# The first FFN of a hybrid block: context products beside latent products on shared weight pages, for half of the tile pairs

## The chip, the cores and the metric

The kernel runs on one core of one Trainium2 chip. Its engines work side by side: TensorE (PE; the loading of its weights is a row of its own, PEld), VectorE (DVE), ScalarE (ACT), GpSimd (POOL) and SyncE (SP), whose queue issues nearly all DMA transfers here. The metric is the device time of one execution in microseconds; of several runs the median counts. Beside the runs there is one profiled execution, from which all rows of the profile come.

## The reference

One layer over 1024 latent tokens and 256 context tokens, D_MODEL = 1024, D_FF = 2816, float32. Cut to what matters here:

```python
def ffn_sublayer(h, shift, scale, gate, g, w_in, w_out):
    hn = modulate(rmsnorm(h, g), shift, scale)
    a, b = jnp.split(hn @ w_in, 2, axis=-1)
    y = (jax.nn.silu(a) * b) @ w_out
    return h + 0.5 * gate[:, None, :] * y

h  = ffn_sublayer(h,  mods[0], mods[1], mods[2], g_ffn1, w_ffn1_in, w_ffn1_out)      # latents
hc = ffn_sublayer(hc, mods_c[0], mods_c[1], mods_c[2], g_ffn1, w_ffn1_in, w_ffn1_out)  # context, same weights
# then projections of both streams, a bidirectional mLSTM, a spatial-gating branch, a merge,
h  = ffn_sublayer(h, mods[6], mods[7], mods[8], g_ffn2, w_ffn2_in, w_ffn2_out)
return rmsnorm(h, g_final)
```

Latents and context pass through the same weights of the first FFN; only the latents pass through the second one.

## The kernel before

**Numbers as pairs.** Every float32 operand of a matmul is split into a high part (a cast to fp32r by ScalarE) and the remainder (a subtraction by VectorE), `split`, L139 to L141. A product is three matmuls: high x high, high x low, low x high. A "page" is a tile of 128 partitions with both parts, `[128, 2, 512]` for the latents' factors and `[128, 2, w]` for weights.

**Latent products in seven steps.** The latent products of both FFNs are computed by a Strassen-like scheme: 1024 x 1024 tokens and channels are taken as 2 x 2 blocks of 512, and seven block products with sums and differences of blocks take the place of eight. `Factors` (L244) makes the factor pages: products 1 and 2 need only the first half of the tokens (`early`), products 5, 6, 7, 4, 3 need differences with the second half (`late`). `Gate` (L287) makes the input products of an FFN. Its 22 output tiles f are taken in pairs (kp, kp + 11); for a tile the steps run in the order `SEQ = (1, 6, 5, 7, 2, 4, 3)`. The first three tiles, the "head", run step by step side by side (`HSEQ`), because their later factors are still being made. A step is one page of weights, split into a ring slot, times four factor pages: 12 matmuls of 128 x 512, all on L351. `Gate.load` issues the load of a tile's two raw pages at its step 1 and forms the sums and differences of weight blocks on POOL in place (L316 to L336); `depth` steps are loaded and split ahead. `Gate.step` (L363 to L387) adds the banks together on VectorE; `Gate.out` (L390) makes the seven factors of the FFN's hidden activation of each pair and stores them, partly already split, to DRAM.

`Out` and `Stage.outp` do the same for the output products: seven products in the order `OSEQ = (1, 2, 4, 7, 6, 5, 3)`, each over 11 pages kp and four rows m, three matmuls each, on L469.

**The context in the first FFN** does not share anything with this. The class `Weights` streams all 44 weight pages of w1i once more, two raw pages and three split pages in flight, and the loop `for f in range(NF)` (L846 to L878) multiplies each with the eight context pages `hnc`: 44 pages x 8 x 3 = 1056 matmuls of 128 x 256 on L166. ScalarE and VectorE form silu(a) * b (L874, L875), split it and store it to `gcsp`. Beside this loop run the statistics, the scaling and the early factor pages of the latents (L804, L192, L193, L238, L239, and the splits). Only then does `A.gate` begin, with the latents in place. After the latents' output products a second loop over the 22 tiles (L970) reads `gcsp` back, loads and splits w1o once more (`wload`, `wsplit`) and makes all eight rows of the context's output: 528 matmuls of 128 x 256. The context's norm follows.

**What sets the order.** Work that need not be done at once is put in the list `todo`. `pump(w)` is called after each group of three matmuls and takes items from it by a credit: an item's cost (512 by default; `slow` and `later` give other values) says how many columns of matmuls lie between two items. `tick` calls do the same for the adaptive-norm weights (`ada_steps`): one load of 256 KB and one or two accumulations on VectorE. The framework's planner then orders the instructions of each engine: the place in the code is the priority, and an instruction that is ready may go ahead of one that is not. Memory is handed out from pools with a fixed number of buffers by tag, and a tile waits until the buffer before it is free.

**Names that the prediction uses.** `raw` (weights as loaded), `hl`, `ring`, `wring` (split weights), `fa`, `fb`, `fc` (factor pages of products 1 and 2, of 5 and 6, and of 7, 4, 3), `qa`, `qb` (banks of `Gate`), `po` (banks of `Out`), `pa`, `pb` (banks of the context's input products), `pc` (of its output rows), `fhl`, `fsp` (stored factors), `adapg` (adaptive-norm weights), `fo` (rows of the result). The last rows are made by `post3`, `fin2` and `put` (L1869 to L1886): a row update and a square for each of four row groups, a norm, and eight rows out, part of them by ScalarE and POOL.

## Time and profile before

| | us |
|---|---|
| median of 3 runs | 2768.88 (2764.06 to 2770.13) |
| the profiled execution, whole | 2752.25 |
| its span (the profile's time axis) | 2750.5 |
| mean granted TensorE clock in it | 0.993 |

A row of a group names the line, the engine, the operation, the tile it writes and those it reads, the count, the busy time with the mean in ns, and the idle time of the engine just before, with what ended it. A row of the timeline begins with start and length in us; one of the waits reads "who <- for whom: us in total, times, longest". In a row of the stretches stand the borders, the length, each engine's busy time with its count of instructions, the granted TensorE clock, the DMA engines' busy share and what they moved in GB/s.

### The profile page before, as it was taken

What the parts mean: (1) busy time and instruction counts of PE and PEld (TensorE: products, weight loads), DVE (VectorE), ACT (ScalarE), POOL (GpSimd) and SP (SyncE); (2) the same over time, 40 slices, a digit from 0 to 9 for tenths busy, and PEclk for the clock granted to TensorE, in tenths of its full rate; (3) what the DMA queues carried; (4) which work ended last, traced back from release to release, by engine and by line L of the source; (5) the groups of instructions that cost most, each with busy time, mean ns of one, the idle gap of its engine ahead of it and who ended that gap; (6) DMA issues with size and microseconds to landing.
All of it is one profiled execution on the core that took longest, in us unless ns stands there. A gap on an engine that the chain in (4) does not pass through costs nothing.

```text
span 2750.5 us, 35573 instructions
## 1 busy us (share of the span) xinstructions
PE 2663.2 (97%) x12652; PEld 2205.5 (80%) x12652; DVE 1946.7 (71%) x3291; ACT 1075.0 (39%) x1826; POOL 589.8 (21%) x551
## 2 busy tenths in 40 slices
PE   8899999999999999999999999999999999999997
PEld 4887788888888878877777888888877788888886
DVE  4887888787968646667665677778478866676755
ACT  3564333334336525453333333112145333333432
POOL 0102232320000121233332315443011323330001
PEclk9999999999999999999999999999999999999999
DMA  8862444439668321236554357547341333337644
GB/s 283 280 202 74 145 146 143 141 132 330 203 212 277 121 92 57 100 129 216 169 175 146 108 176 262 192 164 259 120 138 54 127 127 111 134 119 250 202 159 167
DMA packets 198434, 456.74 MB, mean 166 GB/s; under 512 B 20465, under 2 KB 46833, under 8 KB 198257
## 3 DMA queue, kind: packets, MB, share of 16 engines
q1 hardware_dynamic: 198256, 454.47, 48.4%
q8 instruction: 100, 1.64, 0.2%
q14 instruction: 78, 0.63, 0.1%
HBM read 328.95 MB, written 125.51 MB: 165 GB/s over the span
## 4 chain that ended last, share of the span: by engine, by line
PE 43%; DVE 8%; issue 4%; DMA 3%; POOL 2%; ACT 1%; SPq 0%; POOLq 0%; ACTq 0%; DVEq 0%
PE qb L351 9%; PE pt L1607 9%; PE pq L1180 7%; PE po L469 6%; PE qa L351 4%; PE pr L1099 3%; PE pu L1472 2%; PE pn L1720 2%; DVE ring L141 2%; DMA adapg<-in_w_ada_dram 1%; PE pn L1718 1%; POOL rawq L1146 1%; PE pkc L1160 1%; POOL rawq L1145 1%; DVE adacc L698 1%
## 5 line engine op out<-in xcount | busy, mean ns | idle before, releaser
L140 ACT CAST ring<-rawq 128x512 fp32r<-128x512 f32 x432 | 265.4, 620 | 592.7 <-PE qb L351 146.6
L141 DVE TENSOR_TENSOR ring<-rawq,ring 128x512 fp32r<-128x512 f32 x432 | 332.0, 774 | 213.4 <-ACT ring L140 211.6
L469 PE MATMUL po<-gring,wring 128*128 128x512 f32 x1848 | 422.6, 391 | 2.1 <-DMA gring<-fsp 2.1
L469 PEld LDWEIGHTS po<-gring,wring 128*128 128x128 f32 x1848 | 346.6, 188 | 75.2 <-issue 3.1
L351 PE MATMUL qb<-fc,ring 128*128 128x512 f32 x1440 | 344.3, 393 | 16.6 <-DVE u L371 8.3
L351 PEld LDWEIGHTS qb<-fc,ring 128*128 128x128 f32 x1440 | 272.0, 190 | 76.8 <-DVE y L374 10.6
L351 PE MATMUL qa<-fa,ring 128*128 128x512 f32 x1056 | 253.3, 390 | 0.5 <-ACT ring L140 0.5
L351 PEld LDWEIGHTS qa<-fa,ring 128*128 128x128 f32 x1056 | 198.1, 188 | 42.4 <-ACT ring L140 0.9
L351 PE MATMUL qb<-fb,ring 128*128 128x512 f32 x984 | 229.6, 390 | 0.0
L1180 PE MATMUL pq<-fc,ring 128*128 128x512 f32 x864 | 213.8, 395 | 4.5 <-DVE py L1193 3.4
L351 PEld LDWEIGHTS qb<-fb,ring 128*128 128x128 f32 x984 | 184.9, 188 | 38.2
L1180 PEld LDWEIGHTS pq<-fc,ring 128*128 128x128 f32 x864 | 160.7, 188 | 41.0 <-issue 2.7
L140 ACT CAST wring<-rw 128x512 fp32r<-128x512 f32 x154 | 95.8, 622 | 229.1 <-PE po L469 187.6
L1607 PE MATMUL pt<-yp,ring 128*128 128x512 f32 x768 | 184.3, 397 | 0.0
L141 DVE TENSOR_TENSOR wring<-rw,wring 128x512 fp32r<-128x512 f32 x154 | 108.1, 702 | 95.5 <-ACT wring L140 95.2
L1607 PEld LDWEIGHTS pt<-yp,ring 128*128 128x128 f32 x768 | 144.2, 188 | 29.2
L1180 PE MATMUL pq<-fa,ring 128*128 128x512 f32 x576 | 143.9, 398 | 1.7 <-ACT px L1186 1.5
L1180 PE MATMUL pq<-fb,ring 128*128 128x512 f32 x576 | 138.7, 394 | 1.6 <-DVE ring L141 1.6
L1180 PEld LDWEIGHTS pq<-fa,ring 128*128 128x128 f32 x576 | 108.2, 190 | 25.7 <-ACT px L1186 3.0
L1180 PEld LDWEIGHTS pq<-fb,ring 128*128 128x128 f32 x576 | 107.0, 188 | 26.3 <-DVE ring L141 3.7
L698 DVE SCALAR_TENSOR_TENSOR adacc<-adapg,sc,adacc 128x512 f32<-128x512 f32 x140 | 113.7, 824 | 17.9 <-DMA adapg<-in_w_ada_dram 16.9
L140 ACT CAST ring<-rawt 128x512 fp32r<-128x512 f32 x64 | 39.5, 619 | 185.5 <-PE pt L1607 178.0
(334 smaller groups left out, 4416.9 us busy)
## 6 DMA issues: line engine op xcount, KB each, us to landing
adapg<-in_w_ada_dram SPq DMA_DIRECT2D x144, 256.0 KB, 3.6
fsp<-fhl SPq DMA_DIRECT2D x66, 512.0 KB, 2.8
gring<-fsp SPq DMA_DIRECT2D x66, 512.0 KB, 3.5
raw<-in_w1i_dram SPq DMA_DIRECT2D x44, 512.0 KB, 4.4
graw<-fsp SPq DMA_DIRECT2D x88, 256.0 KB, 3.5
rawq<-in_w1i_dram SPq DMA_DIRECT2D x38, 512.0 KB, 3.8
rawq<-in_w2i_dram SPq DMA_DIRECT2D x38, 512.0 KB, 3.2
fsp<-x SPq DMA_DIRECT2D x66, 256.0 KB, 2.1
```

The source lines that it names most:

```text
L140: S.copy(hl[:, 0, :], src)
L141: V.tensor_sub(hl[:, 1, :], src, hl[:, 0, :].bitcast(F32))
L351: T.matmul(pt, hl[:, x, sl], pages[p][k][:, y, :], start=first and i == 0, stop=i == 11, skip_group_check=not first)
L469: T.matmul(pt, w[:, x, sl], g[:, y, :], start=grp and kp == 0 and i == 0, stop=kp == NFP - 1 and i == 2, skip_group_check=not grp)
L698: eng.scalar_tensor_tensor(acc, pgt, sc2[:, q, k:k + 1], acc, ALU.mult, ALU.add)
L1099: T.matmul(self.pt[m], pg[:, x, sl], hl[:, y, :], start=first and k == 0 and i == 0, stop=k == 3 and i == 2, skip_group_check=not first)
L1145: G.tensor_tensor(b2, b2, b1, ALU.subtract)
L1146: G.tensor_tensor(a1, a1, b2, ALU.add)
L1180: T.matmul(pt, hl[:, x, k * 128:(k + 1) * 128], pg[k][:, y, :], start=first and k == 0 and i == 0, stop=k == 3 and i == 2, skip_group_chec ...
L1472: T.matmul(pu[:, 0:257], ksl[:, kt * 128:(kt + 1) * 128], wv, start=True, stop=True)
L1607: T.matmul(pt, hl[:, x, k * 128:(k + 1) * 128], pg[:, y, :], start=kh + k + i == 0, stop=kh == 1 and k == 3 and i == 2)
L1720: T.matmul(pn[:, 0:257], qi[:, c_, :], self.C[d][:, c_, :], start=False, stop=c_ == 1)
```

## The change

In the first FFN 11 of the 22 tiles ("alone": the two of the head and the last nine) keep their context products in a loop before the latents' products. For the other 11 the context products are made inside `Gate`: the split pages of steps 1, 2 and 4 and of a new step 8 (the block b1 as loaded) are multiplied with the context pages right behind the latent products of the step. The class `Weights` goes; the loop takes half pages from a ring of twelve (four `ring` pages and eight of the second factor pool), with four raw pages, ten half pages ahead. The head has two tiles instead of three, whose raw pages the loop has already loaded.

```diff
     class Gate:
-        def __init__(self, name, raw, ring, depth, sums, pairs, head):
+        def __init__(self, name, raw, ring, depth, sums, pairs, head, alone=None, ctx=None):
...
+            self.alone = fs if alone is None else fs[:head] + fs[2 * pairs + head - alone:]
+            self.steps = [(f, p) for p in HSEQ for f in self.head] + [
+                (f, p) for f in fs[head:] for p in (SEQ if f in self.alone else SEQ[:1] + (8,) + SEQ[1:])]
...
+        def ticks(self, f):
+            if f in self.alone:
+                return (7,) if len(self.alone) < len(self.fs) else (1, 7)
+            return (5,) if self.fs.index(f) < len(self.head) + 3 else (1, 5, 2)
...
+            elif p == 8:
+                src = self.half(f, 1)[0]
...
-            for k in range(4):
+            for k in range(4 if p != 8 else 0):
...
+            if f not in self.alone and p in (1, 2, 8, 4):
+                if p == 1:
+                    self.K[f] = mm_ps("pk")
+                ctx_mm(self.K[f], hl, 0 if p in (1, 2) else 1, 0 if p in (1, 8) else 1)
+                if p == 4:
+                    ctx_out(f, self.K.pop(f))
```

```diff
+    def ctx_mm(pt, hl, j, kh):
+        for k in range(4):
+            for i, (x, y) in enumerate(((0, 0), (0, 1), (1, 0))):
+                T.matmul(pt[:, j * 256:(j + 1) * 256], hl[:, x, k * 128:(k + 1) * 128], hnc[kh * 4 + k][:, y, :],
+                         start=j + kh + k + i == 0, stop=kh == 1 and k == 3 and i == 2, skip_group_check=True)
+            pump(256)
...
+    COVER = 11
+    A = Stage("1", "w1i", 0, True)
...
+    A.q = Gate("w1i", lambda f: rawpg(), A.ring, 4, lambda n: t2(n), NFP, 2, COVER)
...
+    for i, f in enumerate(alone):
...
+        bank = mm_ps("pk")
+        for j in range(2):
+            for kh in range(2):
+                f_, j_, kh_, hl = cready.popleft()
+                ctx_mm(bank, hl, j, kh)
+                cfill(10)
+        ctx_out(f, bank)
...
-    A.gate(A.F.late(fpage, lambda k: []), tick)
+    A.gate(A.F.late(A.fpage, lambda k: [it(n1[1].inplace, k, s0, b0)]), tick)
```

The context pages now stay in memory through the whole of `A.gate`. To make room, the stage's additional ring of three pages goes (`ring2` 3 to 0, so `q.depth` is 4 throughout instead of 7), the page of stored factors `fhl` has one buffer instead of two, and the latents' first rows share their pages with factor 3. The statistics of the latents (`stats`) are paced with cost 640 instead of 1024; the scaling of the second half of the tokens (`n1[1].inplace`) moves from the loop into the late list.

In the output products, products 1 and 2 multiply their split pages also with the stored context activations, which gives rows 0 to 3 of the context's output:

```diff
+                    if gc is not None:
+                        if p == 1 and kp == 0:
+                            cps = [sm_ps("pc") for _ in range(2)]
+                        rows_mm(cps, w, gc, p == 1 and kp == 0, p == 2 and kp == NFP - 1)
+                        if p == 2 and kp == NFP - 1:
+                            self.ctx[1](cps)
```

The loop behind them keeps only rows 4 to 7: it loads and splits the other half of each page of w1o and reads `gcsp` a second time. The context's residual goes through a DRAM buffer `hcsp`, and its norm is made later, in the v projection, whose order is now products 1, 2, 7, 4, 6, 5, then the context's v steps (which load wv a second time), then 3. `Factors.late` makes the factors for these projections in another order (5 and 7 first, then 4, 6 and 3), at cost 1280 instead of 832. In `Rows` product 7 takes the banks that 6 and 5 had, and these those of the others; the vs projection runs in the order `USEQ = (1, 7, 2, 4, 6, 5, 3)`.

The end of the second FFN is changed too. The last four pages of product 3 run in two halves of 256 columns, each with its own norm and rows; the sum of squares is made by matmuls straight from the squares instead of VectorE additions; rows 5 to 7 are scaled ahead by ScalarE and multiplied by POOL, the others by VectorE; the first half of the tokens goes through VectorE alone.

```diff
+                for hx in range(halves if p == 3 else 0):
+                    cs = slice(hx * 512 // halves, (hx + 1) * 512 // halves)
+                    for m, pt in enumerate(pts):
+                        for p_, kp_, w, g, _ in list(self.ready)[:group]:
+                            tile_(pt, kp_, m, w, g, cs)
+                        post3(m, pt, hx, cs)
...
+    class Tail(Norm):
+        def sq(self, d, last):
+            sq = t2("sq")
+            S.activation(sq[:, :self.nt], self.h[d], AF.Square)
+            for j in range(self.nt // 128):
+                T.matmul(self.p4[:, j:j + 1], sq[:, j * 128:(j + 1) * 128], ones[:, 0:1], start=False, stop=last,
+                         skip_group_check=True)
...
     B.outp("w2o", lambda: xpage("raw", "graw", (128, 512)), lambda: B.rpage("gring"), hgate[:, 1, 0, :],
-           bc, lambda n_, d: put(n_, 0, d, d % 4 < P0), fin2, lambda tb, d, t: None)
+           lambda n_: n_.bcast(), lambda n_, d: put(n_, 0, d, False), fin2, lambda tb, d, t: None, halves=2, first=scaled)
```

Within the second FFN's output products `pump` then counts 256 instead of 512 for each group of three matmuls, and the two last groups of items have half their cost.

431 lines of the change are left out of this document (254 added, 177 removed).

## The prediction

> **What bounds the kernel now.** I read the head of the page first, then busy time in stretches cut at the stage borders that the timeline of TensorE shows, then the waits of the first stage.
>
> ```profile
> span 2750.5 us, 35573 instructions
> PE 2663.2 (97%) x12652; PEld 2205.5 (80%) x12652; DVE 1946.7 (71%) x3291; ACT 1075.0 (39%) x1826; POOL 589.8 (21%) x551
> ```
>
> ```profile
> fsp<-fhl SPq DMA_DIRECT2D x66, 512.0 KB, 2.8
> ```
>
> ```profile
> core 0: us, PE busy (x) PEld busy (x) DVE busy (x) ACT busy (x) POOL busy (x), PEclk, DMA share, GB/s
> 8.90:42.30 33.40, 33.40 (x86) 8.20 (x86) 7.61 (x24) 5.96 (x9) 0.73 (x1) 1.00 1.07 363
> 42.30:199.30 157.00, 142.38 (x1094) 135.69 (x1094) 128.78 (x215) 90.65 (x147) 11.77 (x9) 0.98 0.72 235
> 199.30:256.70 57.40, 57.40 (x252) 47.25 (x253) 42.65 (x53) 23.14 (x40) 17.82 (x11) 1.00 0.17 57
> 256.70:300.00 43.30, 35.67 (x148) 28.29 (x148) 42.08 (x59) 16.46 (x30) 13.36 (x8) 0.96 0.54 184
> 300.00:634.40 334.40, 330.74 (x1455) 272.45 (x1454) 261.10 (x372) 115.38 (x196) 93.04 (x63) 1.00 0.43 148
> 634.40:849.50 215.10, 212.87 (x944) 175.57 (x943) 175.54 (x302) 94.40 (x163) 0.00 (x0) 1.00 0.71 239
> 849.50:916.10 66.60, 65.65 (x539) 64.75 (x538) 60.69 (x107) 43.80 (x78) 0.00 (x0) 1.00 0.83 291
> 916.10:1031.00 114.90, 112.30 (x498) 89.06 (x497) 59.13 (x97) 44.27 (x82) 27.95 (x23) 0.99 0.22 79
> 2733.00:2750.50 17.50, 3.12 (x10) 1.47 (x10) 6.53 (x16) 3.26 (x6) 3.72 (x3) 0.64 0.32 120
> ```
>
> The kernel is a stream of matmuls: TensorE is busy in 97% of the span, so a change pays only where it removes matmuls, or where TensorE now stands. The rows are, in order: start-up; the first FFN's context products alone; the head of its latent products (21 steps of three output tiles); the first steps behind the head; the other latent products; the output products; the context's output rows; the v projection and gates; the end. The stretch 42.30 to 199.30 is the worst of the long ones, and its waits say why.
>
> ```profile
> ACT hl L140 <- DMA raw<-in_w1i_dram: 20.3, 18, 3.1
> DVE hl L141 <- ACT hl L140: 14.8, 26, 1.3
> PEld pb L166 <- DVE hl L141: 12.4, 16, 2.1
> ```
>
> Read upwards: the weight loads of TensorE wait for VectorE's half of the split, that for ScalarE's, that for the load; and a load needs one of only two raw pages back from VectorE. It is a round trip through two buffers, with VectorE busy 128.78 of 157.
>
> **Prices.** A matmul of 512 columns in the full stretch: 330.74/1455 = 0.227 us, 2.73 for a step of 12. One of 256 columns: 24 from 65.24 to 68.12, 0.120 us.
>
> ```profile
> 65.24 3.04 PE L166 MATMUL pa<-hnc,hl 128*128 128x256 f32 x24
> 68.12 0.43 PE L166 MATMUL pb<-hnc,hl 128*128 128x256 f32 x2
> ```
>
> ```profile
> 1047.36 1.60 PE L1160 MATMUL pkc<-hnc,ring 128*128 128x256 f32 x12
> 1048.79 2.91 PE L1180 MATMUL pq<-fa,ring 128*128 128x512 f32 x12
> 1051.54 1.59 PE L1160 MATMUL pkc<-hnc,ring 128*128 128x256 f32 x12
> ```
>
> The last three rows are the later k projection, which already mixes context with latent products as the change will: 12 narrow matmuls from 1047.36 to 1048.79, 0.119 each. Mixing makes them no cheaper, so I carry 0.120 on both sides. [...]
>
> **The change, part by part.** It removes no matmul: 11 of 22 tiles keep their 48 context matmuls alone, 11 x 48 = 528 move beside latent products. What goes is 22 loads of 512 KB and their splits, against 11 new half-page splits (step 8).
>
> (1) First stage and head, to the head's last product. The statistics and page splits of the latents, covered by 157 us until now, get only 528 x 0.120 = 63 us of matmuls, so the sum must be made on VectorE.
>
> ```profile
> L141 DVE TENSOR_TENSOR hl<-raw,hl 128x1024 fp32r<-128x1024 f32 x41 | 51.6, 1262 | 14.8 <-ACT hl L140 14.8
> L238 DVE SCALAR_TENSOR_TENSOR h<-h,smod,rb 128x512 f32<-128x512 f32 x16 | 11.8, 740 | 0.0
> L804 DVE TENSOR_TENSOR h<-h,pos 128x512 f32<-128x512 f32 x16 | 11.1, 718 | 1.1 <-DMA h<-in_xT_dram 1.1
> L263 DVE TENSOR_TENSOR h<-h 128x512 f32<-128x512 f32 x16 | 10.7, 687 | 0.0
> L141 DVE TENSOR_TENSOR gc<-sil,gc 128x256 fp32r<-128x256 f32 x21 | 9.9, 474 | 3.3 <-ACT gc L140 3.3
> L193 DVE TENSOR_TENSOR acc<-acc,sq 128x512 f32<-128x512 f32 x14 | 9.6, 689 | 0.8
> L875 DVE TENSOR_TENSOR sil<-sil,pb 128x256 f32<-128x256 f32 x22 | 9.2, 416 | 3.7 <-PE pb L166 2.3 <-issue 1.3
> ```
>
> ```profile
> L768 DVE TENSOR_TENSOR mods<-adc,vec 128x4 f32<-128x4 f32 x6 | 0.7, 157 | 6.8 <-PE adc L764 6.8
> ```
>
> ```profile
> 52.58 1.88 DVE L804 TENSOR_TENSOR h<-h,pos 128x512 f32<-128x512 f32 x3
> ```
>
> VectorE from 42.3 to 256.7 did 128.78 + 42.65 = 171.4. Off go 22 page splits x 1.262 + 11 x (0.416 + 0.474) = 37.6, and the third head tile's 7 splits and 7 sums, 14 x 0.69 (L263, L193) = 9.7. Half-page splits in place of page splits add 44 x 0.69 - 22 x 1.262 = 2.6. Remains 126.7 at mean durations; back to back the engine does better (three in 1.88 us, 0.63 for 0.72 mean), at the least 126.7 x 0.63/0.69 = 115.7. I take the middle, 121, and 10 us of its own waits: the 6.8 on the conditioning stay, those for pages shrink with four raw pages and twelve half-page slots. The head then ends at 42.3 + 131 = 173.3. TensorE's own work would allow 42.3 + 63 + 14 x 2.73 = 144, so VectorE sets it. The fair comparison is 256.7 less what the new kernel does later, 63.4 and one head tile of 7 x 2.73 = 19.1: 174.2. So **-1**. Bounds: 115.7 and 8 of waits, 166 (-8); VectorE no better fed than before (171.4 of 214.4, 80%), 126.7/0.80 = 158 and 201 (+27).
>
> Start-up has two pages instead of three among the conditioning weights while the queue runs at 363 GB/s: 0.52 MB, **-1** (0 to -1.4).
>
> (2) Latent products behind the head. 133 steps x 2.73 = 363 in 377.7: 14.7 lost.
>
> ```profile
> PE qb L351 <- DVE y L374: 8.3, 4, 4.2
> PE qb L351 <- DVE u L371: 3.0, 3, 2.0
> ```
>
> ```profile
> 2164.02 4.79 PE L351 MATMUL qb<-fc,ring 128*128 128x512 f32 x12 [5.29 <-DVE u L371]
> ```
>
> All of it is VectorE behind with the sums; VectorE is busy 42.08 of 43.30 just after the head. Eleven tiles now have 48 x 0.120 = 5.8 us more TensorE work each and 0.69 + 0.89 more on VectorE, so its share falls: (303 + 16 for the extra tile + 17)/(382 + 63) = 76% for 80%. But the new head also carries the scaling of the second half of the latents (8 x 0.74, L238) in the late list, as the second FFN's head does, which stood 5.29. I leave 6 of the 14.7: **-9** (-14 to 0). Added waits: the weight ring is 4 deep instead of 7, raw pages still 4; the head ran on 4 without a gap (57.40 of 57.40), so 0. The stored factor pages go from two buffers to one. A late store (2.8 us) would hold ScalarE's next cast and behind it VectorE's split; the stores are three items of cost 1152 apart, 3 x 1152/512 x 0.68 = 4.6 us, so 0 (to +8 if each of 11 pairs lost 0.7).
>
> (3) Output products and context rows. 264 x 0.120 = 31.7 go to the first two products, 31.7 stay, with some 2 of the norm's matmuls (priced as L199 and L207 in part 4). 33.7 + 31.7 = 65.4 for 66.6. VectorE loses 22 splits, 15; its 60.7 - 15 = 46 now lie over 34 us of matmuls, so 12 us run on beside the first two v products (96 x 0.227 = 21.8, with 8 splits, 5.5): hidden with 4 us to spare. In the first two products DMA gains 22 reads of 256 KB, but they take 31.7 us longer. **-2** (-4 to +8). The context norm leaves the place where 2.6 us stood (112.30 of 114.90) and runs under the later v products; the second reading of wv, 4.2 MB, goes into a stretch at 79 GB/s: **-1** (-2.6 to +3). The new order of the vs products: its stretch shows no idle TensorE, 0.
>
> (4) The end. The last block runs in halves of 256 columns.
>
> ```profile
> 2715.26 5.95 POOL L1872 TENSOR_TENSOR fo<-fo,rbs 128x512 f32<-128x512 f32 x4 [222.16 <-ACT fo L1871]
> 2723.90 9.09 PE L469 MATMUL po<-gring,wring 128*128 128x512 f32 x39 [1.76 <-DMA gring<-fsp]
> 2735.28 1.05 PE L199 MATMUL p<-ones,acc 128*128 128x1 f32 x8 [2.29 <-DVE acc L193]
> 2738.59 2.07 PE L207 MATMUL rb<-diag,ones 128*128 128x512 f32 x2 [2.26 <-DVE diag L203]
> 2741.32 3.38 DVE L1874 SCALAR_TENSOR_TENSOR fo<-h,vec,rb 128x512 f32<-128x512 f32 x5 [2.78 <-ACT rbs L1880]
> 2742.04 3.72 POOL L1872 TENSOR_TENSOR fo<-fo,rbs 128x512 f32<-128x512 f32 x3 [20.83 <-ACT fo L1871]
> ```
>
> From 2733.0 to 2750.5: 2.3 to the sums, 3.3 to the broadcast, 2.7 to the rows, 4.4 for these (to 2745.76), 4.7 for the last store. At half width I price a VectorE or ScalarE step at 0.42, as L875's narrow product above: row update and square without an addition 1.1 with the gaps, sums and root 2.8 (two diagonal blocks of four), broadcast and copy 1.7, five rows x 0.42 = 2.1, store 4.7: 12.4, so -5.1; 96 x 0.120 - 48 x 0.227 = +0.6. The other half's rows leave POOL, where 5.95 us held the store queue and behind it the load that TensorE missed for 1.76: -1.5. **-6** (-8 to +6, the latter if the new sums of squares, matmuls between the row groups, are waited for: 7 x about 1.7).
>
> **Sum.** -1 - 1 - 9 - 2 - 1 - 6 = -20 on a span of 2750.5 (2752.25 with what lies around it). The median of the runs, 2768.88, stands 16.6 above that execution; I carry the difference to it: **2749**.
>
> **The rivals.** *VectorE starves the first stage* (slower). The latents' preparation has 94 us less cover; if VectorE is fed no better than before, the head ends at 201, +27 for -1: 2749 + 28 = 2777. For it: 80% busy then, much of it ACT before DVE. Against: the two-page round trip is gone. It decides once the head ends later than 193. [...]
>
> *All holes fill*: part 1 at 166, no loss behind the head, both ends of 3 and 4: -8 - 1 - 14 - 4 - 3 - 8 = -38, 2731. For it: VectorE falls to 71% in the shared tiles. Against: its bursts at a pair's end stay.
>
> *The loads bind*: 20 pages, x in, x out, the products' stores and the next tile's pages, 10.5 + 4.2 + 4.2 + 2.9 + 1.0 = 22.8 MB, at the stage's 235 GB/s take 97 us of the 131; VectorE waits some 10 more: 2759.
>
> *It only moves work*: no matmul goes, and what the first stage saves comes back as waits in its head; without the gains of 1 and 2 only 3 and 4 remain, -9, and the single factor page takes 6 of its 8: 2766.
>
> **How the numbers follow.** Forecast 0.52, starved 0.15, holes filled 0.15, loads 0.08, only moved 0.10. About 0.2%, 5.5 us, is what a measurement tells from no change: faster is under 2763.3, slower over 2774.4. Faster has the forecast, the filled holes and most of the loads case, 0.73; same the moved case and some, 0.11; slower the starved one, 0.16. The range, 2726 to 2776, reaches to the filled holes and up to the starved case; the forecast's own is 2736 to 2762.
>
> **What would show it.** Right: context products alone over by about 115 to 130, VectorE busy above 90% there, the head done near 173 (wrong if past 190); no wait over 3 us behind it; 0.119 to 0.120 us per narrow matmul beside wide ones; context rows down to 34 us; 13 us from the last product to the end. Wrong, as a whole, if TensorE's idle time before the head's end exceeds 45 us, or if the last block shows matmuls waiting at each row.

## The result and the profile after

The changed kernel takes **2783.4 us** in the median of 5 runs (2776.5 to 2789.3), the kernel before 2768.4 beside it (5 runs): a ratio of 1.0053, 95% interval 1.0039 to 1.0066. It is slower by 15 us; the prediction, 2749 with a range up to 2776, was wrong in sign and in range. The profiled execution of after took 2783.5 us.

The head of the profile of after, then that of a second execution of the kernel before, which took 2763.8 us (the one shown ahead of the prediction took 2752.25, 16 below the median; from here on I compare with this second one):

```profile
span 2780.6 us, 35770 instructions
...
PE 2684.3 (97%) x12734; PEld 2222.9 (80%) x12734; DVE 1909.7 (69%) x3294; ACT 1049.1 (38%) x1820; POOL 580.9 (21%) x550
```

```profile
span 2762.0 us, 35573 instructions
...
PE 2670.8 (97%) x12652; PEld 2207.5 (80%) x12652; DVE 1943.0 (70%) x3291; ACT 1074.7 (39%) x1826; POOL 592.7 (21%) x551
```

TensorE is busy 13.5 us longer. The new end adds 82 small matmuls, and the block that holds them accounts for 5.1 us of this (216.76 for 211.68 in the rows below). So a good part of the loss is not idle time: the same matmuls run slower. The granted clock says it too, 0.985 against 0.992: (1 - 0.985) x 2780.6 - (1 - 0.992) x 2762.0 = 20 us of full clock that after does not get, an upper bound, since a low clock costs nothing where TensorE stands.

Busy time by stretch, cut at the stage borders: first after, then before (second execution). The rows of after are the context alone, the head, the other latent products, the output products with half of the context rows, the other half, the v projection to the first k product, k projection to the vs projection, the output products of the second FFN, and the end.

```profile
41.60:117.70 76.10, 72.60 (x556) 71.28 (x556) 67.53 (x139) 51.59 (x106) 6.21 (x6) 0.93 0.72 247
117.70:177.40 59.70, 46.42 (x181) 33.68 (x180) 54.28 (x90) 26.70 (x48) 15.61 (x10) 0.91 0.17 58
177.40:633.40 456.00, 448.38 (x2213) 379.75 (x2212) 322.90 (x475) 153.82 (x268) 104.81 (x77) 1.00 0.43 145
633.40:887.00 253.60, 247.83 (x1208) 209.28 (x1207) 181.37 (x308) 96.67 (x163) 0.00 (x0) 0.99 0.65 213
887.00:925.30 38.30, 34.96 (x276) 33.07 (x274) 33.80 (x62) 23.48 (x42) 0.52 (x1) 1.00 0.93 317
925.30:1048.90 123.60, 115.52 (x494) 90.98 (x495) 74.31 (x114) 52.00 (x97) 33.07 (x23) 0.96 0.39 129
1048.90:1517.20 468.30, 448.07 (x2023) 364.48 (x2022) 297.66 (x460) 195.78 (x323) 129.26 (x115) 0.97 0.43 142
...
2551.20:2768.40 217.20, 216.76 (x1020) 181.45 (x1019) 143.28 (x242) 85.48 (x153) 2.12 (x3) 1.00 0.60 196
2768.40:2780.60 12.20, 2.15 (x9) 1.26 (x9) 3.83 (x13) 0.99 (x3) 2.09 (x3) 0.58 0.40 132
```

```profile
43.50:204.80 161.30, 145.20 (x1094) 137.27 (x1093) 129.02 (x215) 90.50 (x147) 12.60 (x9) 0.97 0.72 229
...
262.20:639.70 377.50, 366.64 (x1602) 300.64 (x1601) 302.08 (x430) 131.65 (x226) 106.86 (x71) 1.00 0.45 152
639.70:855.80 216.10, 213.60 (x945) 175.44 (x944) 175.33 (x302) 94.32 (x162) 0.00 (x0) 1.00 0.72 238
...
922.90:1036.10 113.20, 110.59 (x497) 87.77 (x496) 59.12 (x97) 44.29 (x82) 27.96 (x23) 1.00 0.23 81
1036.10:1499.20 463.10, 444.78 (x2022) 361.87 (x2021) 295.70 (x458) 195.91 (x323) 130.74 (x115) 0.99 0.43 143
...
2531.30:2744.50 213.20, 211.68 (x935) 174.40 (x933) 140.33 (x225) 84.89 (x146) 5.95 (x4) 1.00 0.61 198
```

After less before, by borders: start-up 41.6 for 43.5, -1.9. First context product to first output product, 591.8 for 596.2, -4.4. First output product to first v product, 291.9 for 283.2, **+8.7**. From there to the first k product, 123.6 for 113.2, **+10.4**. The k stretch, whose work is the same, 468.3 for 463.1, +5.2. Up to the second FFN's output products +1.9. These 217.2 for 213.2, +4.0. The end 12.2 for 17.5, -5.3. Together +18.6 between these two executions; between the medians it is 15. Each stretch here and below comes from one profiled execution, and the same program can differ by 6.6 us in a single stretch, as the first run shows.

### The profile page after: what moved, and what is told of

It reads as the page before. It is cut to its first block, busy times and chain, and to the rows that moved or that the text cites. A ratio compares the mean times of both kernels' runs of the same rounds, so it can differ in the third digit from the quotient of the medians.

```text
span 2780.6 us, 35770 instructions
## 1 busy us (share of the span) xinstructions
PE 2684.3 (97%) x12734; PEld 2222.9 (80%) x12734; DVE 1909.7 (69%) x3294; ACT 1049.1 (38%) x1820; POOL 580.9 (21%) x550
## 4 chain that ended last, share of the span: by engine, by line
PE 45%; DVE 7%; issue 4%; DMA 2%; POOL 2%; ACT 1%; SPq 0%; POOLq 0%; DVEq 0%; ACTq 0%
PE qb L362 9%; PE pq L1295 9%; PE pt L1757 8%; PE po L494 6%; PE qa L362 4%; PE pr L1214 3%; PE pu L1621 2%; PE pn L1870 2%; DVE ring L109 1%; DMA adapg<-in_w_ada_dram 1%; PE pn L1868 1%; PE pkc L1275 1%; POOL rawq L1261 1%; POOL rawq L1260 1%; ACT ring L108 1%
## 5 line engine op out<-in xcount | busy, mean ns | idle before, releaser
L109 DVE TENSOR_TENSOR ring<-rawq,ring 128x512 fp32r<-128x512 f32 x453 | 338.5, 752 | 238.4 <-ACT ring L108 233.7
L108 ACT CAST ring<-rawq 128x512 fp32r<-128x512 f32 x453 | 277.6, 620 | 570.1 <-PE qb L362 160.1
L494 PE MATMUL po<-gring,wring 128*128 128x512 f32 (+1 forms) x1896 | 429.2, 385 | 1.1 <-DMA gring<-fsp 0.4
L362 PE MATMUL qb<-fc,ring 128*128 128x512 f32 x1464 | 352.3, 393 | 12.9 <-DVE u L391 12.9
L1295 PE MATMUL pq<-fc,ring 128*128 128x512 f32 x864 | 220.2, 403 | 8.0 <-DVE py L1308 5.7
L346 POOL TENSOR_TENSOR rawq<-rawq 128x512 f32<-128x512 f32 x41 | 55.9, 1365 | 294.2 <-DVE ring L109 294.2
```

Of the source, the lines that this page charges most:

```text
L108: S.copy(hl[:, 0, :], src)
L109: V.tensor_sub(hl[:, 1, :], src, hl[:, 0, :].bitcast(F32))
L346: G.tensor_tensor(a2, a2, a1, ALU.subtract)
L362: T.matmul(pt, hl[:, x, sl], pages[p][k][:, y, :], start=first and i == 0, stop=i == 11, skip_group_check=not first)
L494: T.matmul(pt[:, cs], w[:, x, sl], g[:, y, cs], start=grp and kp == 0 and i == 0, stop=kp == NFP - 1 and i == 2, skip_group_check=not grp)
L1295: T.matmul(pt, hl[:, x, k * 128:(k + 1) * 128], pg[k][:, y, :], start=first and k == 0 and i == 0, stop=k == 3 and i == 2, skip_group_chec ...
```

## The experiments

Ratios are to the kernel before, run beside each. The second and third rows start from the kernel before, all later ones from the changed kernel.

| edit | median, us | ratio, 95% interval |
|---|---|---|
| the change itself | 2783.4 | 1.0053, 1.0039 to 1.0066 |
| before, once more | 2764.8 | 0.9994, 0.9980 to 1.0008 |
| before with the new end alone | 2766.2 | 0.9998, 0.9987 to 1.0009 |
| no sharing of pages | 2771.3 | 1.0013, 1.0002 to 1.0025 |
| no position values | 2769.9 | 1.0009, 0.9996 to 1.0021 |
| norm sums of the latents later | 2778.1 | 1.0032, 1.0019 to 1.0044 |
| half of the low parts on GpSimd | 2782.7 | 1.0048, 1.0035 to 1.0061 |
| all context rows in the second pass | 2778.1 | 1.0040, 1.0026 to 1.0054 |
| context pages on GpSimd's queue | 2776.4 | 1.0030, 1.0021 to 1.0040 |
| first loads in the general ring | 2778.1 | 1.0036, 1.0022 to 1.0050 |
| ... and on GpSimd's queue | 2781.6 | 1.0046, 1.0031 to 1.0061 |
| ... with the context pages too | 2783.0 | 1.0060, 1.0043 to 1.0076 |
| context norm's sums later | 2773.4 | 1.0021, 1.0009 to 1.0033 |
| four differences on VectorE | 2777.4 | 1.0038, 1.0024 to 1.0053 |
| twelve differences on VectorE | 2773.1 | 1.0012, 1.0001 to 1.0023 |
| three edits together, loads on SyncE | **2759.6** | **0.9963**, 0.9950 to 0.9976 |
| ... on GpSimd's queue | 2767.2 | 0.9989, 0.9977 to 1.0001 |
| another three, loads on GpSimd's queue | 2766.0 | 0.9995, 0.9984 to 1.0006 |
| ... on SyncE | **2759.2** | **0.9970**, 0.9958 to 0.9982 |

### The kernel before, once more

> The kernel before, unchanged, profiled once more. Theory A (the profiled execution of before was a lucky one: the half-clock stretches of TensorE, 24 us of them between 42 and 2740 us, depend on where short waits fall): another execution shows 40 us or more of half clock and a span of 2760 or more, and the stretch from the first k-projection product to the first vs product, 456.6 us in the first profile, is 4 to 10 us longer although the order of instructions is the same. Rival B (the clock is a property of the kernel): 24 us of half clock again, span 2750, 456 to 458 us.

Its rows are those shown above, and theory A held in its times, with a span of 2762.0 us; its reason, where short waits fall, these rows do not show. The k stretch took 456.5 us at clock 1.00 in the first execution and 463.1 at 0.99 in this one, with the same program:

```profile
1031.00:1487.50 456.50, 439.30 (x2022) 358.42 (x2021) 296.74 (x459) 195.85 (x323) 129.83 (x115) 1.00 0.43 145
```

So a difference of 5 us in that stretch is no cost of the change that one could point to. Over all profiles of this study it lies between 456.5 and 469.4, the longest belonging to a version that beats after as a whole; whether the change makes it long more often is not shown: the three profiles of before and of before with the new end have 456.5 to 463.2, the seventeen of after and its variants 460.3 to 469.4.

### The new end alone

The kernel before, with the halves, the sums of squares by matmuls and the new sharing of the last rows.

> The kernel before with the new end of the second FFN alone. Theory: the end from the last product shrinks from 17.5 to 12.4 as in the changed kernel and the halves cost 3 to 4 us in the products ahead, so 1 to 3 us faster than before. Rival (the added sums of squares, matmuls between the row groups, eat all of it): no difference or slower by up to 4.

End 11.6 us for 17.5, but the products ahead of it 216.9 for 213.2, and no measurable gain. In after one sees where it goes (timeline of TensorE):

```profile
2756.70 0.50 PE L230 MATMUL p<-ones,sq 128*128 128x1 f32 x4
2757.07 0.72 PE L494 MATMUL po<-gring,wring 128*128 128x256 f32 x4
...
2769.41 0.61 PE L230 MATMUL p<-ones,sq 128*128 128x1 f32 x4 [0.69 <-ACT sq L228]
```

They are not waited for, as I had feared: only 0.69 us behind the last square. But four sums of one column cost 2757.07 - 2756.70 = 0.37 us, and eight such groups stand between products, 3.0 us. With the broadcast of the first half, 0.5, and the halved matmuls, 0.6, this makes 4.1 us for the +4.0 of that block. A wait for a load there is also 1.1 us shorter than in before, so about 1 us stays unexplained.

### No sharing

```diff
-    COVER = 11
+    COVER = 22
```

All 22 tiles make their context products ahead of the latents', in the changed kernel's memory and with its ring of half pages.

> The changed kernel with all 22 tiles' context products alone again (still half pages, four raw pages, ring of twelve, head of two): none beside latent products. Theory V (VectorE is the limit until the head's end; sharing pages saves VectorE's splits but the cover is lost as well, so the input stage gains nothing): first output product at 633 +- 6 us, as in the changed kernel and before, total within 6 us of the changed kernel. Rival S (sharing pays as it saves 22 page loads and splits): the first output product comes 10 to 20 us later, total 10 to 20 us slower than the changed kernel.

```profile
42.70:189.80 147.10, 140.78 (x1093) 138.81 (x1093) 131.29 (x263) 101.02 (x199) 7.57 (x6) 0.94 0.69 228
189.80:230.20 40.40, 38.64 (x170) 31.42 (x169) 37.19 (x48) 11.71 (x21) 18.00 (x11) 1.00 0.56 179
230.20:622.30 392.10, 384.47 (x1686) 316.53 (x1685) 307.30 (x435) 137.25 (x234) 106.37 (x75) 1.00 0.45 149
```

From the first context product to the first output product it takes 579.6 us, for 591.8 in after and 596.2 in before. Neither forecast came about: the first output product is 11 us earlier, not at the same time and not later. Up to this border the rest of the change (more raw pages, half pages, the smaller head, the other pacing, none of them tried alone) gains 16.6 us, and the sharing gives 12.2 of it back. But the border moves: the output products then wait and take 293.8 us. From the first context product to the first v product it is 873.4 us without sharing, 883.7 in after, 879.4 in before (873.8 in its first execution). So the sharing costs 10 to 12 us, which the medians confirm (2771.3 for 2783.4), and of the gain of the rest at most 6 us are left there. Where the sharing loses: up to the head's end the matmuls at the prices of the prediction are 1056 x 0.120 + 14 x 2.73 = 164.9 of 187.5 without sharing (22.6 lost), and 528 x 0.120 + 38.2 = 101.6 of 135.8 with it (34.2 lost): 11.6. Behind the head 392.1 - 140 x 2.73 = 9.9 are lost without sharing and 456.0 - 382.2 - 63.4 = 10.4 with it. The wide cover of narrow matmuls behind the head bought nothing.

### VectorE in the first stage

Three runs. The first leaves out the 16 additions of the latents' position values.

```diff
-            slow(add_pos, tb, d, cost=640)
```

> The changed kernel without the addition of the position embedding (16 VectorE additions of 128x512, 16 x 0.69 = 11 us, left out). Theory V (VectorE sets the end of the head, 177.4 us): the head ends 8 to 12 us earlier and the first output product 6 to 12 us earlier, the total likewise. Rival C (the order on TensorE sets it: the norm's matmuls wait for the sums while ready products stand behind them): the head ends less than 4 us earlier.

The head ends 126.5 us after the first context product, 135.8 in after: -9.3 for 16 additions of some 0.68 us. The second run puts the norm sums of the second half of the latents nine places later in TensorE's order, because after shows a wait for them, and slow matmuls behind it, thirteen at 0.384 us for 0.227:

```profile
117.73 1.55 PE L362 MATMUL qa<-fa,ring 128*128 128x512 f32 x6
126.40 1.84 PE L167 MATMUL p<-ones,acc 128*128 128x1 f32 x8 [7.12 <-DVE acc L162]
128.10 4.99 PE L362 MATMUL qa<-fa,ring 128*128 128x512 f32 x13
```

```diff
-        todo.extend([nop, n1[tb].rstd, nop, nop, n1[tb].bcast])
+        todo.extend([nop] * (10 if tb else 1) + [n1[tb].rstd] + [nop] * 2 + [n1[tb].bcast])
```

> The norm sums of the second half of the latents are put nine places (about 6 us of matmuls) later in the first stage's order. Theory of a wait: the 7.12 us wait just behind the start of the latent products and the half clock behind it are a cost of the order, the head ends 5 to 10 us sooner (gate start to head end 59.6 -> 50 to 55), and the time falls by 5 to 10 us against 2783. Rival, the theory of VectorE: the head's end is set by VectorE's work (the run without position additions moved it by 9.3 us with 9.6 us of additions left out), so the wait only moves to another place: the head end stays within 3 us of 135.8 us after the first context product, and the time within 3 us of 2783.

```profile
132.53 1.20 PE L180 MATMUL rb<-diag,ones 128*128 128x512 f32 x2 [1.94 <-DVE diag L176]
...
139.54 6.72 PE L362 MATMUL qb<-fb,ring 128*128 128x512 f32 x20 [1.77 <-ACT fb L108]
```

The wait of 7.12 is down to 0.95, and others stand in its place; the head ends at 138.2 us after the first context product, no sooner. VectorE sets it.

Why the sums are late in after can be read from its trace. From 114.3 to 127.4 us GpSimd forms sums and differences of weight blocks, eight operations back to back, and beside them VectorE takes up to 1.78 us for what takes it 0.69 elsewhere:

```profile
120.67 3.37 POOL L344 TENSOR_TENSOR rawq<-s,rawq 128x512 f32<-128x512 f32 x2
```

```profile
121.17 1.75 DVE L162 TENSOR_TENSOR acc<-acc,sq 128x512 f32<-128x512 f32 x1
```

Seven operations of VectorE between 114.66 and 126.25 us lose 7.2 us in all, as much as TensorE waits. In before the same additions took 689 ns (L193 in the prediction), ahead of GpSimd's work. No run moved GpSimd's operations here, so this is a reading of the trace; the v projection below has the test of the same link.

The third run gives GpSimd every second low part of the context's pages:

```diff
-        split(hl, craw[f, j][:, kh * 512:(kh + 1) * 512])
+        src = craw[f, j][:, kh * 512:(kh + 1) * 512]
+        S.copy(hl[:, 0, :], src)
+        (G if cring[0] % 2 else V).tensor_tensor(hl[:, 1, :], src, hl[:, 0, :].bitcast(F32), ALU.subtract)
```

> Half of the low parts of the first stage's split pages (those of the context alone, about 22 subtractions of 0.6 us) are made by GpSimd instead of VectorE. Theory: VectorE sets the first stage; with some 13 us of work off it the head ends 6 to 13 us sooner after the first context product (135.8 -> 123 to 130) and the time falls by 5 to 12 us against 2783. Rival: GpSimd holds VectorE up while it runs, as in the v projection, and is slower itself: the head ends at 132 to 145 and nothing is gained.

The head ends at 139.6. Groups of VectorE up to there, first of this run, then of after (count, busy us, mean ns):

```profile
L894 DVE TENSOR_TENSOR hl<-rawc,hl 128x512 fp32r<-128x512 f32 x16 | 16.1, 1012 | 1.8 <-ACT hl L893 1.8
L916 DVE TENSOR_TENSOR h<-h,pos 128x512 f32<-128x512 f32 x14 | 13.8, 995 | 0.2 <-DMA h<-in_xT_dram 0.2
```

```profile
L109 DVE TENSOR_TENSOR hl<-rawc,hl 128x512 fp32r<-128x512 f32 x32 | 21.3, 705 | 1.7 <-ACT hl L108 1.7
...
L914 DVE TENSOR_TENSOR h<-h,pos 128x512 f32<-128x512 f32 x14 | 9.5, 684 | 0.0
```

Half of the instructions left VectorE, but of 21.3 us only 5.2, because the rest run at 1012 ns instead of 705; the position additions, which nobody touched, lose 4.3. From 42 to 118 us GpSimd is busy for 31.6 of the 76 us, in after for 6.5, and these two groups of VectorE are 44 and 45% longer in the mean.

### The output products: rows or loads

In after the output products start badly. SyncE's queue, then TensorE; beside them SyncE in before:

```profile
632.88 0.33 SPq L627 DMA_DIRECT2D fsp<-x  x1
...
639.14 1.97 SPq L460 DMA_DIRECT2D graw<-fsp  x3
```

```profile
648.68 4.39 PE L528 MATMUL pc<-gc,wring 128*128 128x256 f32 x19 [3.92 <-DMA gc<-gcsp]
```

```profile
637.17 0.33 SPq L439 DMA_DIRECT2D graw<-fsp  x1
...
639.07 0.33 SPq L561 DMA_DIRECT2D fsp<-x  x1
```

In before the loads of the gate's results (`graw`) go out ahead of a late store (`fsp<-x`), in after behind it. 19 narrow matmuls in 4.39 us behind the wait, 0.231 each for 0.119, are at half clock: the granted clock is 0.50 from 648.7 to 653.0. First the context rows were taken away from there, all eight into the second pass with whole pages, as before (the outline of the edit):

```diff
-           lambda tb, d, t: nc.sync.dma_start(hsp[tb, d], t), tick, ctx=(gpage, ctx_lo))
+           lambda tb, d, t: nc.sync.dma_start(hsp[tb, d], t), tick)
...
-    pcs = [sm_ps("pc") for _ in range(2)]
+    pcs = [mm_ps("pc") for _ in range(4)]
```

> All eight context output rows are again worked in the second pass, with whole pages of the output weights loaded and split a second time, as before; the first stage's half of the change, the new memory layout, the store of the context rows and the end stay. Theory: the output half is the larger part of the loss: its stretch (first output to first v product) goes from 291.9 back to 281 to 285 us and the time falls by 6 to 11 us, to 2772 to 2777, with the k projection's stretch still long (120 to 125). Rival: the rows beside the products do save work, the stretch grows or stays (290 to 300) and the time is 2780 to 2790; the loss is then all in the first stage and the norm.

```profile
652.89 47.49 PE L494 MATMUL po<-gring,wring 128*128 128x512 f32 x195 [12.75 <-ACT gring L108]
```

The stretch grew to 301.9 instead of shrinking. Without the rows, which had filled the time, the late operands stand as one wait of 12.75 us. So in this stretch the rows beside the products save some 10 us in this memory, and what costs comes with the layout or the order, not with them. The whole run was no slower than after (2778.1), because the v projection took 118.1 us for 123.6 and the k stretch 460.3 for 468.3; why is not known. Four runs then tried to bring the loads forward. The context pages' loads on another queue:

```diff
-        nc.sync.dma_start(g.bitcast(F32), gcsp[f // 2, :, f % 2])
+        nc.gpsimd.dma_start(g.bitcast(F32), gcsp[f // 2, :, f % 2])
```

> Only the queue of the context pages' loads in the first output products (and in the second pass of context rows) changes: GpSimd's instead of SyncE's. Theory: TensorE waits 5.6, 4 and 3.9 us there because these loads stand in SyncE's order behind other loads and stores that wait for VectorE; then those waits fall under 1 us each, the stretch from the first output product to the first v product goes from 291.9 us back to 280 to 287, and the time falls by 4 to 8 us against the changed kernel (2783). Rival: two buffers, freed by TensorE itself, or the traffic of the loads set these waits; then the stretch stays within 2 us of 291.9 and the time within 3 us of 2783.

The stretch stayed, 292.9. The run was faster than the change for another reason: the next stretch took 118.0 us for 123.6. Nearly all of this lies ahead of the norm, whose wait of 5.4 us stands as before: the first 96 v products ran without a wait, where after waits 3.6 us for split pages and part of them runs slow. Why is open. Then other buffers for the first loads:

```diff
-        if grn[0] < 3:
-            return A.rg.tile([128, 512], F32, name="graw", tag="sums", bufs=2)
+        if grn[0] < 6:
+            return t2("graw")
```

> Only the buffers of the first five loads of the gate's results in the output products change: the general ring of twelve in place of two of the sums' buffers, the store's single buffer and the new pages, all of which the gate itself holds until its last product. Theory: the output stretch is long because these loads are issued 6 to 10 us after they were in the kernel before (at 639 to 653 us instead of 624 to 643, behind a store that waits 6.8 us for VectorE), which with all rows moved away showed as one wait of 12.75 us and 20 us at half clock: the stretch from the first output product to the first v product falls from 291.9 to 281 to 287 us, and no wait of over 2 us is left in its first 30 us; the time falls by 5 to 10 us against 2783. Rival: the waits are those of the context pages' two buffers (3.9 us) and stay: the stretch stays within 2 us of 291.9.

The stretch fell to 287.2, but the first output product came 5.1 us later (596.9 for 591.8 from the first context product), behind a wait of 5.4: nothing gained. With these five loads on GpSimd's queue as well:

```diff
-                nc.sync.dma_start(g, self.fsp[p][kp])
+                early = self.ctx is not None and p == 1 and kp < 5
+                (nc.gpsimd if early else nc.sync).dma_start(g, self.fsp[p][kp])
```

> The first five loads of the gate's results in the output products are issued from GpSimd's queue instead of SyncE's (into the general ring, as in the run before that moved the buffers). Theory: they came late because of SyncE's order alone (behind the store of a product's result, which waits 6.4 us for VectorE): the first output product starts at 632 to 635 us, no wait of over 2 us stands in the 30 us behind it, the stretch from the head's end to the first v product (747.9 in the changed kernel, 748.5 with the buffers moved) falls to 738 to 744, and the time is 2770 to 2776. Rival: the buffers still come free too late, or the gate's last results are made too late whatever the queue: 746 to 749 and no gain.

Now TensorE waited 7.9 us for the context's page, which stands behind the same store. With that moved too:

> As grawq, and the first five context pages (and three of the second pass) are loaded from GpSimd's queue too. Theory: SyncE's order was the only cause: the first output product starts at 632 to 636 us, TensorE waits less than 2 us in all between 630 and 660, the stretch from the head's end to the first v product (747.9 in the changed kernel, 751.2 in grawq) falls to 738 to 744 and the time is 2770 to 2776. Rival: VectorE and ScalarE, which make the gate's last results at that time, set the start whatever the queue: 746 to 750, no gain.

The first three pages were issued at 623 to 626 us, and it still did not help; two waits of 4.1 us remain. ScalarE casts the first three operands only behind one of the gate's last casts (`fhl`, at 639.85), and VectorE finishes them behind the gate's last results, one of which itself waits 3.52 us for a store:

```profile
640.37 1.65 ACT L108 CAST gring<-graw 128x512 fp32r<-128x512 f32 x3
```

```profile
643.94 0.69 DVE L420 TENSOR_TENSOR x<-x,ft 128x512 f32<-128x512 f32 x1 [3.52 <-DMA fsp<-x]
...
645.15 0.69 DVE L109 TENSOR_TENSOR gring<-graw,gring 128x512 fp32r<-128x512 f32 x1
```

So SyncE's order alone is not the cause: even with the loads early, the casts and subtractions lie behind the gate's last results, on two engines. Why is open. Without sharing, the stretch is as long, 293.8; the layout (no additional ring of three pages, one store page) is what these runs have in common, but it was not tried alone.

### The v projection: GpSimd beside the norm

In after the context norm's additions (min/median/max in ns, then the first and last start), a third of the twelve operations that GpSimd runs back to back beside them, then TensorE's wait for the additions, and last the same additions in before:

```profile
L162 DVE TENSOR_TENSOR acc<-acc,sq x7: 413/1303/1502, 965.5 to 974.8; 128x256 f32<-128x256 f32 x7
```

```profile
L1196 POOL TENSOR_TENSOR raw<-raw,rawq x4: 1285/1367/1735, 956.5 to 969.6; 128x512 f32<-128x512 f32 x4
```

```profile
975.27 1.01 PE L167 MATMUL p<-ones,acc 128*128 128x1 f32 x4 [5.37 <-DVE acc L162]
976.15 3.76 PE L1214 MATMUL pr<-ring,fc 128*128 128x512 f32 x8
```

```profile
L193 DVE TENSOR_TENSOR acc<-acc,sq x8: 410/416/684, 859.8 to 927.1; 128x256 f32<-128x256 f32 x7, 128x512 f32<-128x512 f32 x1
```

The same addition takes three times as long, and eight matmuls behind the wait 3.76 us for some 1.8, at a granted clock of 0.50 from 976 to 980. First the sums were put later in TensorE's order:

```diff
-    todo.extend([nop, nct.rstd, nop, hc_bcast])
+    todo.extend([nop] * 10 + [nct.rstd] + [nop] * 3 + [hc_bcast])
```

> The context norm's sums are put ten places (about 7 us of matmuls) later in TensorE's order, inside the v projection; nothing else changes. Theory: the 5.37 us wait of TensorE for the last slow addition of the norm, and the half clock behind it, make most of the 10 us that the stretch from the first v product to the first k product has gained (113.2 before, 123.6 after): it falls to 114 to 119, the time by 5 to 9 us against 2783. Rival: the stretch is long because of the ring's waits and VectorE's work as a whole: then it stays at 121 to 125.

The wait is gone and the stretch is 117.0: 6.6 us. The additions are as slow as before. The first try at their cause moved the differences of product 7 from GpSimd to VectorE:

> The four first differences of weight blocks in the v projection run on VectorE instead of GpSimd; nothing else changes. Theory: GpSimd's differences of 1.3 to 1.7 us, back to back, are what makes five of the context norm's additions take 1.4 us each instead of 0.42; without them each of the five takes under 0.6 us, TensorE's wait of 5.37 us for the sums goes to under 2, and the stretch from the first v product to the first k product falls from 123.6 to 115 to 120. Rival: the additions are slow for another reason (transfers at 0.93 of their engines' time in that stretch, ScalarE's squares): they stay over 1 us, and the stretch, with 2.5 us more work on VectorE, is 122 to 128.

(`(V if self.name == "wv" else G)` at product 7.) A miss: those run earlier, the additions stayed at 1304 ns and the stretch did not move. The twelve that lie beside the additions are those of products 6, 5 and 3:

```diff
-                G.tensor_tensor(b2, b2, b1, ALU.subtract)
+                E.tensor_tensor(b2, b2, b1, ALU.subtract)
...
+            E = V if self.name == "wv" else G
```

> The twelve differences of weight blocks that GpSimd makes beside the context norm's additions in the v projection (those for the last products) run on VectorE instead; nothing else changes. Theory: GpSimd holds VectorE up there: each of the five additions goes from 1.44 us to under 0.6, although VectorE has 8 us more of its own work, TensorE's wait of 5.37 us for the sums falls under 3, and the stretch from the first v product to the first k product is 116 to 122 (123.6 in the changed kernel). Rival: the additions are slow for another reason and stay over 1 us, and the 8 us more of work make the stretch 124 to 130.

```profile
L162 DVE TENSOR_TENSOR acc<-acc,sq x7: 416/417/425, 966.4 to 971.7; 128x256 f32<-128x256 f32 x7
```

```profile
926.90:1042.20 115.30, 112.80 (x497) 88.73 (x496) 73.75 (x126) 51.37 (x96) 14.50 (x11) 0.99 0.41 138
```

All seven at 417 ns, no wait, 115.3 for 123.6. VectorE is busy 73.75 us, 74.31 in after, although it does twelve subtractions more: what GpSimd took over cost VectorE as much as doing it. This link is shown: the three versions with this edit take 113.7 to 115.3 us in this stretch, the eleven without it and without the sums put later 118.0 to 124.3.

### Together

No sharing, the norm's sums later, the first loads in the general ring:

> Three edits at once: the context tokens of all pairs alone ahead of the latents (no sharing of split pages), the norm's sums later in the v projection, the first loads of the output products in the general ring. If the three losses are separate they add: 12 us, 6.6 us and 5 to 10 us off 2783, so 2755 to 2762, 5 to 12 us under the kernel before (2767). If the half clock only moves to other places: 2764 to 2772, no gain over before.

2759.6. The same with the loads on GpSimd's queue:

> The three edits of the run that beat the kernel before (2759.6 at 2768.9) and the five loads on GpSimd's queue. If the late loads still cost there (a wait of 6.8 us for the first output product's operand): 2752 to 2757. Rival: 2758 to 2763, no difference.

2767.2: the other queue loses what was gained. No sharing, twelve differences on VectorE, the general ring, and both kinds of loads on GpSimd's queue:

> Context of all pairs alone ahead of the latents, the v projection's twelve differences on VectorE, and the first loads of the output products on GpSimd's queue. If the losses add (12, 10 and 4 to 8 us off 2783): 2753 to 2758, 10 to 15 us under the kernel before (2769). Rival: the queue gains nothing: 2758 to 2763.

2766.0, again no better than before. Without the other queue:

> The same without the other queue: all loads on SyncE, the first five of the gate's results in the general ring. If the losses of sharing and of GpSimd's differences add: 2757 to 2762, as the run with the norm's sums put later (2759.6). Rival: one hides the other: 2763 to 2768.

2759.2, with TensorE busy 2674.4 us, 9.9 less than in after. Two versions beat the kernel before by 0.3 to 0.4%. Both leave the pages unshared. What they gain over the run that only stops sharing lies in the v projection, 116.3 and 113.7 us for 124.3. The general ring gained nothing there: from the first context product to the first v product they take 875.4 and 875.6 us, for 873.4 without it. That the losses add, as expected, is therefore not shown, though the times fell in the forecast range; no run has the first two edits without the general ring.

## Why the prediction was wrong, step by step

**(1) First stage and head, -1 forecast.** Right in its place and nearly in its size. One row for the whole of it:

```profile
41.60:177.40 135.80, 119.02 (x735) 104.96 (x735) 121.81 (x228) 78.29 (x152) 21.82 (x15) 0.92 0.48 164
```

VectorE is busy 121.8 us (121 forecast) and waits 14.0 (10 forecast); the context products are over at 117.7, the head at 177.4 for 173.3, so +3.2 on the comparison point of 174.2 (which comes from the first execution of before; in the second the head ends 4.3 us later after the first context product). That 121 came so near is partly luck: it was the middle of two bounds, 115.7 and 126.7. That VectorE sets it is shown by the runs without position values and with later sums. The start-up gained 1.9. The rival of a starved first stage, with its border at 193, did not come about. What the step missed is what stands behind GpSimd: the norm's sums, on which TensorE waits 7.12 us. It also missed the alternative: the changed kernel without sharing is 12 us better.

**(2) Behind the head, -9 forecast.** Mis-sized. By the prediction's prices 10.4 us are lost for 6 forecast, 14.5 in before: -4. The argument that eleven wider tiles lower VectorE's share and so its lateness failed: the share fell further than forecast, to 322.90 of 456.00, 71%, and the loss stayed; without sharing it is 9.9. TensorE still waits for the sums at each pair's end, which is a burst, not a share:

```profile
PE qb L362 <- DVE u L391: 7.6, 5, 2.7
```

**(3) Output products, rows, norm, -2 and -1 forecast.** This is the step that failed, +8.7 and +10.4, beyond both upper bounds. (Its own figures, 65.4 for 66.6, give -1.2 and not -2.) The price of a narrow matmul was right, and the run without the rows shows that they save in this stretch. But the products with rows took 253.6 us, where 216.1 and 31.7 make 247.8, and the rows behind them 38.3 for 33.7. On the price, 12 narrow matmuls among wide ones go from 667.69 to 669.12, 0.119 each:

```profile
667.69 1.59 PE L528 MATMUL pc<-gc,wring 128*128 128x256 f32 x12
669.12 2.91 PE L494 MATMUL po<-gring,wring 128*128 128x512 f32 x12
```

Two things were not in the sum. The norm "runs under the later v products", I wrote, as if that place were free; there GpSimd makes twelve differences, and I gave that no price: 8.3 us, shown by taking the differences away. No row of before shows it in this place, but the head of before had it, three subtractions in 4.09 us beside GpSimd, for 0.69 each alone:

```profile
200.61 4.09 DVE L141 TENSOR_TENSOR ring<-rawh,ring 128x512 fp32r<-128x512 f32 x3
```

And the output products' operands come late, with single waits of 4 to 13 us, depending on what fills the time; the rows show the place, the cause is not settled.

**(4) The end, -6 forecast.** From the last product to the end -5.3, as worked out. The block ahead was forecast at -0.9 and came at +4.0: the sums as matmuls cost 3.0 there in TensorE's own time, where I had feared only that they be waited for. The run with the end alone nets zero.

**The clock** was in no term. Up to 20 us of full clock were not granted, as much as the whole 18.6, and the clock is lower in the stages that gained a wait: 0.93 and 0.91 in the first stage for 0.97 and 1.00, 0.96 in the v projection for 1.00. This is why a wait can cost more than its length: behind the 5.37 us at the context norm eight matmuls take 3.76 us for 1.8, and the whole came to 6.6 us when only the sums were moved, 8.3 when the differences were. What follows a wait should have been asked of every added one: even a wait of 1.86 us is followed by slow matmuls (twelve in 4.58 us, in the last rows). In the k stretch, with the same work, 5.2 us come at 0.97 for 0.99 and cannot be told from luck.

**The median.** Adding the sum to the median rather than to the fast profiled execution was right; the error is all in the sum. The chance for slower, 0.16, hung on one mechanism in the first stage; the loss came from places where I had put all moves at about zero.

## What to carry to other kernels

Work that is moved has to be priced beside its new neighbours: what GpSimd runs beside VectorE there, and whose loads, casts and subtractions it now lies behind. Where TensorE is 97% busy, a new wait can cost more than its length, here up to about twice (the two rows at the end: 1.86 us of waiting, and 1.6 us more in twelve matmuls behind it), so a change that removes no matmul must remove waits. And try the buffers without the idea they were made for: here the shared pages were a loss of 10 to 12 us, and the two versions that beat the kernel before do without them.

## What was not expected of the hardware

An addition of 128 x 256 with two inputs took 417 ns on VectorE alone and 1303 in the median beside GpSimd, which ran operations of 1.3 to 1.7 us back to back. The same program took 2752 and 2764 us in two profiled executions, 6.6 of it in one stretch of the same matmuls, at clock 1.00 and 0.99. A short wait can be followed by slow matmuls, and need not be. The same twelve matmuls of the k projection behind the same wait, first in the first profiled execution of before, then in after:

```profile
1240.59 2.99 PE L1180 MATMUL pq<-fc,ring 128*128 128x512 f32 x12 [1.88 <-DVE py L1193]
```

```profile
1260.88 4.58 PE L1295 MATMUL pq<-fc,ring 128*128 128x512 f32 x12 [1.86 <-DVE py L1308]
```

The granted clock is 1.00 in the first (1240.5 to 1243.6 us) and 0.64 in the second (1260.8 to 1265.5). What decides between the two no run here shows. Two executions of before, the same program, took 456.5 us at clock 1.00 and 463.1 at 0.99 in the stretch that holds the first of these rows.
